# A tile of its own for a half result, and operand sums one weight block later

## The chip, the cores and the metric

One core of a Trainium2 chip runs the whole kernel. The metric is device time in microseconds (us) of one execution. TensorE (PE) multiplies, VectorE (DVE) and ScalarE (ACT) do elementwise work and read PSUM, GpSimd (POOL) does elementwise work on SBUF, and SyncE (SP) and ScalarE issue the DMAs.

## The reference

One decoder layer on 1024 tokens of width 1024, in float32: two token mixers side by side, gated and merged, then a gated MLP with a causal convolution of width 3.

```python
xn = rmsnorm(x, norm_mix_w)
da_q, da_k, da_v, sw_q, sw_k, sw_v, g_da, g_sw = split_cols(xn @ w_in)
y_da = diff_attention(da_q, da_k, da_v, lam, lam_init, subln_w)   # 4 heads, causal
y_sw = sliding_window_attention(sw_q, sw_k, sw_v, sinks)          # 8 heads, window 128
merged = sigmoid(g_da) * (y_da @ w_br_da) + sigmoid(g_sw) * (y_sw @ w_br_sw)
x = x + merged @ w_mix_out
xn = rmsnorm(x, norm_ffn_w)
u = xn @ w_up
c = conv_b + sum(shift(u, 2 - j) * conv_w[j] for j in range(3))
gate, val = split(c)
x = x + (silu(gate) * val) @ w_down                               # 2816 hidden columns
out = rmsnorm(x, norm_final_w)
```

## The kernel before

Activations lie transposed, channels on partitions and tokens along the free dimension; a product makes a 128x512 PSUM bank (128 output channels, half of the tokens). To keep float32 accuracy each operand is split into a high part (a cast to fp32r on ScalarE) and a low part (source minus high, on VectorE), and a product takes three matmuls: high by high, low by high, high by low. Weights come in blocks of 128 output channels: a DMA on SP into a tile "raw" (three buffers), a cast to "wh" (L132, two buffers), a low part "wl" (L134). `next_w` hands out the next block and prepares the one behind it. Some products use Strassen-Winograd's seven products for a two by two block product; their operands are sums and differences of weights (on GpSimd) and of activations (on VectorE).

The kernel is traced as one program by a framework that inserts all waits. It also chooses each engine's order before the run: of the instructions that it expects to be ready it takes the one traced first, so work can pass work that was traced ahead of it. Tiles of one pool and tag share that tag's buffers. `tc.issue_after(ins)` adds edges: what its block traces on the engine of `ins` is queued behind `ins`.

**The second attention** (`sw_step`, called from `attention` for units u = 4 and 5, eight steps each) takes four heads of 128 queries against two key blocks. A step makes scores (L707), a minimum and exponentials (L714, L716), a scaling (L721), transposes (L728), splits (L731, L732) and the value product (L738) into one PSUM bank. That product's lower 64 partitions hold the high parts of the values, the upper 64 the low parts; the upper half is copied by ScalarE to a tile (L740) and added to the lower one by VectorE in two instructions (L745) into "ys", which goes to memory.

Between the steps `back_half` works on the gates' projections that are left over: a half is 24 matmuls (L153 to L155) into one of two PSUM banks of the tag "g", a copy by ScalarE (L548) to an SBUF tile of the tag "g", and a DMA to memory. HALVES says how many halves follow each step (one behind steps 0, 2, 4, 6 of u = 4 and behind 2, 4, 6 of u = 5, four more behind the attention). The tile for L740 is of the same pool and tag as the gates' tile: two buffers in all. The first attention's norm (`da_norm`) keeps squares in a tile of the tag "sq" of the pool `ap`, one buffer, 512 elements wide. Behind the attention `rest` reads the results back ("yr", split into "yh" and "yl" by L806 and L807) and multiplies them by the branch weights.

**The down product** (`down`) takes 22 hidden row blocks j. The first 6 go as ordinary products in 16 pieces (L1083). The next 8 go as Strassen-Winograd products: four weight blocks m = 0..3 with B11 and B21 (the loop around L1112, on L887), then for each of four pairs the five products with T1, T2, B22, T3 and T4. The last 8 are ordinary again (L1056). `sums_h(k)`, for k = 0..3, loads four 128x512 pieces "hr" (L980, nine buffers), makes four differences in place on VectorE (L996, L998, L999, L1002) and splits them into T1 to T4 (cast L806, low part L807). `preps` are the splits of the operands that need no sum. The sums are traced at the last piece (k = 0) and behind the weight blocks m = 0, 1, 2 (k = 1, 2, 3). The weight that is prepared while block m is handed out is block m + 1, and for m = 3 the half weight A22.

Of the kernel before, what the change touches and what calls it, by code (L numbers as in the profile page):

```python
# [17 lines left out]
P = 128  # L18
# [24 lines left out]
class Trunk:  # L43
# [652 lines left out]
    def sw_step(self, g, n, st):  # L696
        nc, ap = self.nc, self.ap
        q, k = st
        k0 = max(n - 1, 0) * P
        w = P if n == 0 else 256  # L700
        bo = T + (P if n == 0 else 0)
        sc = self.tl(self.psS, [P, 4, 256], "sc")
        s = self.tl(self.st, [P, 4, 4], "sw", bufs=4)
        L = self.tl(ap, [P, 4, 256], "L", bufs=4)
        for h in range(4):
            for part in range(2):
                nc.tensor.matmul(sc[:, h, :], q[h][:, n * P:(n + 1) * P], k[part][:, k0:k0 + 256], start=part == 0, stop=part == 1)  # L707


        a, at, we = (0, w, w + 1) if n == 0 else (1, 0, w)  # L710
        nc.gpsimd.tensor_copy(L[:, :, at:at + 1], self.nsink[:, 4 * g:4 * g + 4].unsqueeze(2))
        for h in range(4):
            slope, ns = 2.0 ** -(4 * g + h + 1), self.nsink[:, 4 * g + h:4 * g + h + 1]
            nc.vector.tensor_tensor_reduce(L[:, h, a:w], sc[:, h, a:w], self.bias[:, bo + a:bo + w], slope, ns, ALU.add, ALU.min, s[:, 0, h:h + 1])  # L714
        for h in range(4):
            nc.scalar.activation(L[:, h, :we], L[:, h, :we], AF.Exp, bias=s[:, 0, h:h + 1], scale=-1.0, accum_out=s[:, 2, h:h + 1])  # L716
        nc.vector.reciprocal(s[:, 3, :], s[:, 2, :])
        if n:
            nc.gpsimd.memset(L[:, :, 0:1], 0.0)
        for h in range(4):  # L720
            self.last = nc.vector.tensor_scalar(L[:, h, a:w], L[:, h, a:w], s[:, 3, h:h + 1], None, ALU.mult)  # L721
        po = self.tl(self.psT, [P, H2], "t")
        nblk = w // P
        parts = []
        for b in range(nblk):
            ps = self.tl(self.psT, [P, 4, P], "t")
            for h in range(4):
                nc.tensor.transpose(ps[:, h, :], L[:, h, b * P:(b + 1) * P], self.ident)  # L728
            pt = self.tl(ap, [P, 2, 4, P], "aT", F32R, bufs=5)
            hi, lo = pt[:, 0], pt[:, 1]  # L730
            nc.scalar.copy(hi, ps)  # L731
            nc.vector.tensor_tensor(lo, ps, hi.bitcast(F32), ALU.subtract)  # L732
            parts.append((hi, lo))
        for b, (hi, lo) in enumerate(parts):
            kb = k0 // P + b
            va = self.vsw[kb // 4][:, kb % 4, g]
            for m, pt in enumerate((hi, lo)):
                nc.tensor.matmul(po, va, pt, start=b == 0 and m == 0, stop=b == nblk - 1 and m == 1)  # L738
        t = self.tl(self.gpool, [P, 4, P], "g", bufs=2)[0:64]
        nc.scalar.copy(t, po[64:128].rearrange("p (h q) -> p h q", h=4))  # L740
        pv = po[0:64].rearrange("p (c e q) -> p c e q", c=2, e=2)
        tv = t.rearrange("p (c e) q -> p c e q", e=2)
        y = self.tl(ap, [P, 2, P], "ys", bufs=3)
        for e in range(2):
            nc.vector.tensor_tensor(y[64 * e:64 * e + 64], pv[:, :, e], tv[:, :, e], ALU.add)  # L745
        self.store(self.yd[4 + 2 * g:6 + 2 * g, :, n * P:(n + 1) * P].rearrange("c p q -> p c q"), y)
# [288 lines left out]
    def down(self):  # L1035

        nc, tc = self.nc, self.tc
        with ExitStack() as ctx:
# [28 lines left out]
            sums = [lambda k=k: self.sums_h(k) for k in range(4)]  # L1067
            pss = {}
            n = N1 // 2
            for i, (m, c) in enumerate(self.pieces):  # L1070
                if i % 2 == 0:
                    with tc.high_priority(150 if i < 4 else 0):
                        w2 = self.next_w()
                w = [v[:, i % 2 * n:i % 2 * n + n] for v in w2]
                lo = self.lo
                for hf in range(2):
                    if c == 0:
                        pss[m, hf] = bank(hf)
                    js = range(n * c, n * c + n)
                    for q, j in enumerate(js):  # L1080
                        h, l = self.hs[hf, j]
                        for p, (v, x) in enumerate(((w[0], h), (w[0], l), (w[1], h))):
                            nc.tensor.matmul(pss[m, hf], v[:, q, :], x, start=c == q == p == 0, stop=c == 1 and q == n - 1 and p == 2 and (m > 3 or hf > 0))  # L1083
                if i in (2, 8):
                    ms = slice(4 - i // 8 * 4, 8 - i // 8 * 4)
                    nc.sync.dma_start(x3[:, ms], self.x2d[ms].rearrange("m p t -> p m t"))
                for _ in range(n if i < 2 else 1):
                    if preps:
                        preps.pop(0)()
                if i in DEFER:  # L1090
                    self.defer.pop(0)(lo)
                if i in STORE:

                    with tc.issue_after(self.load.ins):
                        self.late.pop(0)()
                if i == len(self.pieces) - 1:
                    sums.pop(0)()
                if c == 1:

                    for hf in range(m < 4, 2):  # L1100
                        x = col(m, hf)
                        tt(x, x, pss[m, hf], ALU.add)
            assert not preps
            ys = []
            for m in range(4):
                wh, wl = self.next_w()
                y, ps = bank(1), pss[m, 0]
                ys.append(y)
                self.product(y, (wh[:, 0:4], wl[:, 0:4]), "B11", skip=True, low=True)
                self.product(ps, (wh[:, 4:8], wl[:, 4:8]), "B21", first=False)  # L1110
                for p in (y, ps):
                    tt(col(m, 0), col(m, 0), p, ALU.add)  # L1112
                if sums:
                    sums.pop(0)()
            late = [(hf, j) for hf in range(2) for j in range(N1 + 8, NF)]
            for m, y in enumerate(ys):
                w = self.next_w()
# [23 lines left out]
            def evac(ps, m, hf, a=0, b=H2):  # L1141

                x = x3[:, m, hf * H2 + a:hf * H2 + b]
                tt(x, x, ps, ALU.add)
                sum_ = acc[:, hf, a:b]
                sq = sum_ if m == 0 else self.tl(self.uw, [P, b - a], "sl")
                nc.scalar.activation(sq, x, AF.Square)
                if m and (m < KC - 1 or not hf):
                    tt(sum_, sum_, sq, ALU.add)
                nc.scalar.mul(x, x, self.vecs[:, C_NO + m:C_NO + m + 1])  # L1150
                return sq
# [15 lines left out]
            for a, b in ((0, q), (q, H2)):  # L1167
                for m, w in ws:
                    ps = bank(m % 2)[:, :q]
                    mms(ps, w, 1, js, a, b, lambda n, m=m: tail.pop(0)() if a and n == (4 if m < KC - 1 else 2) else None)  # L1170
                    sq = evac(ps, m, 1, a, b)
# [100 lines left out]
```

## Time and profile before

| | |
|---|---|
| median of 3 runs | 1345.15 us (1344.61 to 1345.49) |
| the profiled execution | 1344.88 us, span 1343.0 us |
| granted TensorE clock, mean | 0.997 |
| PE busy | 1326.8 us, 99% |
| DVE busy | 1052.5 us, 78% |
| ACT busy | 602.3 us, 45% |
| POOL busy | 488.8 us, 36% |
| HBM | 133 GB/s over the span |

Profile times count from the first instruction of the span. The second attention's steps run from about 400 to 490 us, the branch products behind them from 502, the pieces of down from about 1099 and its four blocks of B11 and B21 from 1164.6. In a row of the profile "y<-h,wh" means: writes tile y, reads h and wh. The engine names PEld and SPq stand for TensorE's weight loads and SyncE's queue.

### The profile page before, as it was taken

What the parts mean: (1) busy time and instruction counts of PE and PEld (TensorE: products, weight loads), DVE (VectorE), ACT (ScalarE), POOL (GpSimd) and SP (SyncE); (2) the same over time, 40 slices, a digit from 0 to 9 for tenths busy, and PEclk for the clock granted to TensorE, in tenths of its full rate; (3) what the DMA queues carried; (4) which work ended last, traced back from release to release, by engine and by line L of the source; (5) the groups of instructions that cost most, each with busy time, mean ns of one, the idle gap of its engine ahead of it and who ended that gap; (6) DMA issues with size and microseconds to landing.
All of it is one profiled execution on the core that took longest, in us unless ns stands there. A gap on an engine that the chain in (4) does not pass through costs nothing.

```text
span 1343.0 us, 17167 instructions
## 1 busy us (share of the span) xinstructions
PE 1326.8 (99%) x6304; PEld 1105.7 (82%) x6304; DVE 1052.5 (78%) x1425; ACT 602.3 (45%) x929; POOL 488.8 (36%) x364
## 2 busy tenths in 40 slices
PE   8999999999999999999999999999999999999997
PEld 6888888888888878888888888888888888788886
DVE  7846775388898976445669999999999998967454
ACT  8432232276667774344444434343434345432433
POOL 0346652000101016642446566666666611131011
PEclk9999999999999999999999999999999999999998
DMA  7244443966554245324522222222222239642342
GB/s 258 108 146 162 148 149 119 273 170 189 143 148 144 70 155 206 141 95 130 167 79 95 79 79 85 88 79 79 88 85 80 86 128 320 220 145 98 94 141 79
DMA packets 63812, 179.49 MB, mean 134 GB/s; under 512 B 7024, under 2 KB 16880, under 8 KB 63728
## 3 DMA queue, kind: packets, MB, share of 16 engines
q1 hardware_dynamic: 52272, 161.22, 36.8%
q10 hardware_dynamic: 11456, 17.18, 3.5%
q8 instruction: 50, 0.82, 0.2%
q14 instruction: 34, 0.28, 0.1%
HBM read 129.61 MB, written 48.76 MB: 133 GB/s over the span
## 4 chain that ended last, share of the span: by engine, by line
PE 72%; DVE 15%; issue 8%; DMA 2%; ACT 1%; POOL 1%; SPq 0%; POOLq 0%; DVEq 0%; ACTq 0%
PE t L887 24%; PE g L153 4%; PE g L154 4%; PE g L155 4%; DVE c L1031 3%; PE y L1056 3%; PE d L1056 3%; PE sc L154 3%; PE sc L155 3%; PE sc L153 3%; PE d L887 3%; PE sc L619 3%; PE y L887 2%; DVE wl L113 2%; DMA hr<-hd 2%
## 5 line engine op out<-in xcount | busy, mean ns | idle before, releaser
L1020 POOL TENSOR_TENSOR us<-us,rstd 128x1024 f32<-128x1024 f32 x42 | 92.6, 2225 | 85.0 <-DVE us L452 47.6
L1029 ACT ACTIVATE c<-us,vecs 128x1024 f32<-128x1024 f32 x44 | 54.8, 1248 | 118.3 <-POOL us L1020 113.8
L132 ACT CAST wh<-raw 128x1024 fp32r<-128x1024 f32 (+2 forms) x58 | 58.7, 1012 | 107.9 <-PE sc L154 35.8
L134 DVE TENSOR_TENSOR wl<-raw,wh 128x1024 fp32r<-128x1024 f32 (+2 forms) x58 | 78.3, 1352 | 32.5 <-ACT wh L132 22.8
L113 DVE TENSOR_TENSOR sl<-sf,sh 128x1024 fp32r<-128x1024 f32 x62 | 89.3, 1442 | 12.8 <-ACT sh L111 12.8
L111 ACT CAST sh<-sf 128x1024 fp32r<-128x1024 f32 x62 | 64.5, 1042 | 61.6 <-PE t L887 44.0
L97 POOL TENSOR_TENSOR sf<-rv 128x512 f32<-128x512 f32 x30 | 51.3, 1711 | 93.6 <-DVE sl L113 51.1
L1031 DVE SCALAR_TENSOR_TENSOR c<-us,vecs,c 128x1024 f32<-128x1024 f32 x44 | 75.4, 1746 | 2.7 <-ACT c L1029 2.7
L99 POOL TENSOR_TENSOR sf<-raw,rv 128x512 f32<-128x512 f32 x30 | 56.7, 1891 | 46.3 <-DVE sl L113 46.3
L1032 DVE SCALAR_TENSOR_TENSOR c<-us,vecs,c 128x1024 f32<-128x1024 f32 x44 | 73.2, 1696 | 0.0
L153 PE MATMUL g<-xh,wh 128*128 128x512 f32 x176 | 71.0, 403 | 1.5 <-ACT g L548 1.5
L154 PE MATMUL g<-xl,wh 128*128 128x512 f32 x176 | 70.3, 400 | 0.0
L155 PE MATMUL g<-xh,wl 128*128 128x512 f32 x176 | 70.3, 399 | 0.0
L170 POOL TENSOR_TENSOR rs<-ms,mhalf 128x8 f32<-128x8 f32 (+2 forms) x9 | 13.5, 1499 | 155.5 <-DVE ms L168 149.4
L1012 ACT ACTIVATE c<-c 128x1024 f32<-128x1024 f32 x22 | 23.4, 1064 | 89.6 <-DVE c L1032 89.6
L113 DVE TENSOR_TENSOR wl<-raw,wh 128x1024 fp32r<-128x1024 f32 (+1 forms) x35 | 61.8, 1765 | 0.3 <-ACT wh L111 0.2
L602 POOL MEMSET aT<- 128x128 f32 x32 | 6.1, 204 | 151.5 <-PE t L648 101.2
L623 DVE CUSTOM_DVE_ANT_0 L<-sc,bias 128x128 f32<-128x128 f32 (+7 forms) x64 | 47.8, 752 | 16.6 <-PE sc L619 13.7
L98 POOL TENSOR_TENSOR sf<-sf,raw 128x512 f32<-128x512 f32 x31 | 58.2, 1877 | 2.2
L624 ACT ACTIVATE L<-L,sm 128x128 f32<-128x128 f32 (+7 forms) x64 | 49.6, 778 | 20.0 <-DVE sm L623 17.3
L776 POOL TENSOR_TENSOR gr<-gr,rstd 128x1024 f32<-128x1024 f32 x16 | 40.3, 2523 | 43.9 <-DMA gr<-gd 43.7
L113 DVE TENSOR_TENSOR wl<-rv,wh 128x512 fp32r<-128x512 f32 x30 | 54.0, 1800 | 2.6 <-ACT wh L111 2.6
(435 smaller groups left out, 4338.4 us busy)
## 6 DMA issues: line engine op xcount, KB each, us to landing
u<-qd SPq DMA_DIRECT2D x72, 256.0 KB, 6.4
raw<-in_w_down SPq DMA_DIRECT2D x27, 512.0 KB, 3.7
hr<-hd SPq DMA_DIRECT2D x50, 256.0 KB, 4.8
raw<-in_w_up SPq DMA_DIRECT2D x23, 512.0 KB, 3.5
raw<-in_w_in SPq DMA_DIRECT2D x22, 512.0 KB, 3.8
hd<-c SPq DMA_DIRECT2D x22, 512.0 KB, 2.6
rv<-in_w_up SPq DMA_DIRECT2D x21, 512.0 KB, 3.5
gr<-gd SPq DMA_DIRECT2D x16, 512.0 KB, 3.4
```

What stands on the lines that cost most here:

```text
L111: cast = nc.scalar.copy(hi, src)
L113: low = nc.vector.tensor_tensor(lo, src, hi.bitcast(F32), ALU.subtract)
L132: self.hi = nc.scalar.copy(wh, raw)
L134: self.lo = (eng or nc.vector).tensor_tensor(wl, raw, wh.bitcast(F32), ALU.subtract)
L153: nc.tensor.matmul(ps, wh[:, kc + o, :], ah, start=first and n == 0, stop=False)
L154: nc.tensor.matmul(ps, wh[:, kc + o, :], al, start=False, stop=False)
L155: nc.tensor.matmul(ps, wl[:, kc + o, :], ah, start=False, stop=last and n == len(kcs) - 1)
L887: nc.tensor.matmul(ps, (ah, ah, al)[p][:, k, :], (bh, bl, bh)[p], start=first and n == p == 0, stop=last and p == 2 and n == len(ks) - 1, ...
L1020: i = (nc.vector if m % NF == 0 else nc.gpsimd).tensor_tensor(us[:, 2:], us[:, 2:], self.rstd, ALU.mult)
L1031: nc.vector.scalar_tensor_tensor(c, us[:, 1:T + 1], cw[1], c, ALU.mult, ALU.add)
L1032: nc.vector.scalar_tensor_tensor(c, us[:, 0:T], cw[0], c, ALU.mult, ALU.add)
L1056: nc.tensor.matmul(ps, v[:, n, :], x, start=n == i == 0, stop=n == len(js) - 1 and i == 2)
```

## The change

In `sw_step` the tile for the half result comes from the pool `ap` under the tag "sq" with one buffer, where it came from the gates' pool under the tag "g" with two. In `down` the sums for k = m are traced at the beginning of the weight block m, behind `next_w` and ahead of its products; none is traced at the last piece. Each block of sums is put behind `self.hi`, the cast of the weight prepared last, which concerns its casts on ScalarE alone.

```diff
@@ sw_step
-        t = self.tl(self.gpool, [P, 4, P], "g", bufs=2)[0:64]
+        t = self.tl(ap, [P, 4, P], "sq", bufs=1)[0:64]
         nc.scalar.copy(t, po[64:128].rearrange("p (h q) -> p h q", h=4))
@@ down
                         self.late.pop(0)()
-                if i == len(self.pieces) - 1:
-                    sums.pop(0)()
                 if c == 1:
...
             for m in range(4):
                 wh, wl = self.next_w()
+
+                with tc.issue_after(self.hi.ins):
+                    sums.pop(0)()
                 y, ps = bank(1), pss[m, 0]
                 ys.append(y)
                 self.product(y, (wh[:, 0:4], wl[:, 0:4]), "B11", skip=True, low=True)
                 self.product(ps, (wh[:, 4:8], wl[:, 4:8]), "B21", first=False)
                 for p in (y, ps):
                     tt(col(m, 0), col(m, 0), p, ALU.add)
-                if sums:
-                    sums.pop(0)()
```

## The prediction

> **What bounds the kernel now.** I read the page first, then the waits of TensorE over the whole span, then the timelines of the two places that the change touches. The page's first row, and the waits view (who waited for whom: total us, times, longest us):
>
> ```profile
> PE 1326.8 (99%) x6304; PEld 1105.7 (82%) x6304; DVE 1052.5 (78%) x1425; ACT 602.3 (45%) x929; POOL 488.8 (36%) x364
> ```
> ```profile
> PE t L280 <- ACT wh L310: 5.0, 1, 5.0
> PE g L153 <- ACT g L548: 1.5, 4, 0.5
> ...
> PE y L887 <- DVE wl L134: 0.5, 1, 0.5
> PE t L738 <- DVE aT L732: 0.4, 1, 0.4
> PE y L887 <- ACT wh L132: 0.3, 1, 0.3
> ...
> PE d L1083 <- DVE wl L134: 0.2, 1, 0.2
> PE t L728 <- DVE ys L745: 0.2, 1, 0.2
> ```
>
> TensorE is busy 99% of the span, so a change that neither adds nor removes matmuls can gain only what TensorE waits. The first row above is the kernel's start, which the change does not touch. The others shown lie in the two places that it does touch: the second attention (L153 on g, L738, L728) and the first part of down (L1083, L887). Together they are 3.1 us. That is the stock from which a gain can come; a loss has no such limit.
>
> **The first edit: the half result's tile.** The columns of a timeline are start, busy time, engine, line, operation, and in brackets the idle time before it with what ended it.
>
> ```profile
> 410.11 0.58 ACT L740 COPY g<-t 64x512 f32<-64x512 f32 x1 [1.49 <-PE t L738]
> 410.72 0.59 ACT L548 COPY g<-g 128x512 f32<-128x512 f32 x1
> ...
> 487.91 0.58 ACT L740 COPY g<-t 64x512 f32<-64x512 f32 x1 [1.51 <-DMA yd<-ys]
> ...
> 488.58 0.59 ACT L548 COPY g<-g 128x512 f32<-128x512 f32 x1
> ```
> ```profile
> 411.36 0.50 PE L153 MATMUL g<-xh,wh 128*128 128x512 f32 x1 [0.25 <-ACT g L548]
> ...
> 484.61 0.50 PE L153 MATMUL g<-xh,wh 128*128 128x512 f32 x1 [0.50 <-ACT g L548]
> ...
> 509.93 0.39 PE L153 MATMUL g<-yh,wh 128*128 128x512 f32 x1
> ```
>
> Between 408 and 490 us ScalarE makes eight gate copies (L548), and each stands directly behind a half-result copy (L740); the first and the last pair are shown. Both write a tile of the tag "g", two buffers handed out in program order, and in the program the gate's tile follows the step's. So a finished gate half sits in its PSUM bank until the step's last matmul (L738) is done and L740 has run. There are two such banks; four times TensorE needs one back and waits, 1.5 us in all by the waits view, 0.25 the first time and 0.50 the last. With the half result in a tile of its own, L548 can go as soon as its half is ready, and these four waits go.
>
> A wait costs more than the idle time shown, because a matmul's modelled end lies behind the moment at which the next could start. The row of eight at 1164.58 (below) takes 1.98 us, a single one 0.39 (509.93 above): (1.98 - 0.39) / 7 = 0.227 us from start to start, so 0.39 - 0.23 = 0.16 us of the last one's time is normally overlapped and is lost at each wait. I take the same tail for the transposes and score matmuls that precede these waits. The edit is worth 1.5 + 4 x 0.16 = 2.1 us.
>
> The edit also adds a wait: the new tag has one buffer, so L740 must follow the two adds (L745) that read the half result of the step before. Below are the two that stand nearest to each other in the rows that I read, and the last reader of the same tag in the stage before:
>
> ```profile
> 405.14 0.95 PE L161 MATMUL t<-ones,sq 128*128 128x1 f32 x8
> ```
> ```profile
> 448.22 0.85 DVE L745 TENSOR_TENSOR ys<-t,g 64x256 f32<-64x256 f32 x2
> ```
> ```profile
> 451.17 0.58 ACT L740 COPY g<-t 64x512 f32<-64x512 f32 x1 [0.38 <-PE t L738]
> ```
>
> The adds end at 449.07, the next copy starts at 451.17: 2.1 us of cover, so I cost this at nothing. If VectorE fell behind by more than that, each excess would stand on ScalarE ahead of the casts and exponentials queued there. The tag is the one in which the first attention's norm keeps its squares; their last reader, L161, ends at 406.1, so the first step's copy at 410.11 finds it free.
>
> What comes next when TensorE stops waiting? The sixteen steps keep VectorE busy too:
>
> ```profile
> 408.00:490.00 82.00, 79.97 (x452) 66.25 (x451) 74.33 (x240) 59.44 (x161) 8.29 (x27) 1.00 0.36 116
> ```
> ```profile
> 505.25 2.44 DVE L807 TENSOR_TENSOR yl<-yr,yh 128x1024 fp32r<-128x1024 f32 x2 [0.69 <-ACT yh L806]
> ```
>
> In the windows view the columns behind the length are the busy times of TensorE (79.97 of 82), its weight loads, VectorE (74.33), ScalarE and GpSimd. So the steps may end no sooner than now, near 489 us, and the gain appears only as less gate work left over behind them. That work hides the trip of the last result through memory. Its last low part ends at 505.25 + 2.44 = 507.69 and its first reader is the fourth row block of the branch product, at 509.93: 2.24 us of slack. If the trip doesn't move at all, 2.1 of gain still fits, barely. The other two waits of this stage (L738, L728: 0.4 and 0.2, with tails 0.9 us) come from VectorE and I leave them in.
>
> **The second edit: the operand sums.** Rows of ScalarE, TensorE, VectorE, GpSimd and the SP queue, one of the windows view, and two of the page's DMA rows (size, median us to landing):
>
> ```profile
> 1139.33 0.62 ACT L806 CAST h<-hr 128x512 fp32r<-128x512 f32 x1 [2.09 <-DVE hr L996]
> ...
> 1148.45 4.27 ACT L806 CAST h<-hr 128x512 fp32r<-128x512 f32 x8
> ...
> 1161.56 1.04 ACT L132 CAST wh<-raw 128x1024 fp32r<-128x1024 f32 x1
> 1167.08 2.40 ACT L806 CAST h<-hr 128x512 fp32r<-128x512 f32 x4 [4.48 <-DVE hr L999]
> 1169.39 1.04 ACT L132 CAST wh<-raw 128x1024 fp32r<-128x1024 f32 x1
> ...
> 1176.82 1.06 ACT L132 CAST wh<-raw 128x1024 fp32r<-128x1024 f32 x1 [0.36 <-ACT wh L132]
> 1182.22 0.62 ACT L132 CAST wh<-raw 128x512 fp32r<-128x512 f32 x1 [4.34 <-PE d L887]
> ```
> ```profile
> 1164.58 1.98 PE L887 MATMUL y<-h,wh 128*128 128x512 f32 x8
> ...
> 1170.48 2.11 PE L887 MATMUL y<-h,wh 128*128 128x512 f32 x8 [0.30 <-ACT wh L132]
> 1173.05 1.20 PE L887 MATMUL y<-h,wl 128*128 128x512 f32 x4 [0.45 <-DVE wl L134]
> ...
> 1189.73 0.61 PE L887 MATMUL d<-h,sh 128*128 128x512 f32 x2
> ```
> ```profile
> 1156.53 2.88 DVE L807 TENSOR_TENSOR h<-hr,h 128x512 fp32r<-128x512 f32 x2
> ...
> 1168.16 2.49 DVE L807 TENSOR_TENSOR h<-hr,h 128x512 fp32r<-128x512 f32 x4
> ...
> 1183.05 0.69 DVE L134 TENSOR_TENSOR wl<-raw,wh 128x512 fp32r<-128x512 f32 x1
> ```
> ```profile
> 1157.13 1.73 POOL L98 TENSOR_TENSOR c<-c,raw 128x512 f32<-128x512 f32 x1
> ...
> 1185.19 1.31 POOL L97 TENSOR_TENSOR c<-raw 128x512 f32<-128x512 f32 x1 [24.63 <-DMA raw<-in_w_down]
> ```
> ```profile
> 1190.00:1200.00 10.00, 10.00 (x46) 8.29 (x45) 5.12 (x8) 2.11 (x2) 3.27 (x3) 1.00 0.31 107
> ```
> ```profile
> 1151.93 0.33 SPq L122 DMA_DIRECT2D raw<-in_w_down  x1
> ```
> ```profile
> raw<-in_w_down SPq DMA_DIRECT2D x27, 512.0 KB, 3.7
> hr<-hd SPq DMA_DIRECT2D x50, 256.0 KB, 4.8
> ```
>
> The 512 KB weights of the four blocks are cast by the 128x1024 rows of L132, the first at 1161.56, the second at 1169.39, the fourth at 1176.82; the row at 1182.22 is the half weight behind them. The second was asked for at 1151.93 and landed near 1155.6; its buffer came free when the last piece ended, at 1164.58. Yet its cast ran at 1169.39, because ScalarE stood 4.48 us before a cast of an operand sum, L806, that waited for VectorE's subtraction L999. TensorE paid 0.30 for the high part and 0.45 for the low part. The change orders every cast of a block's sums behind the cast of the next weight, so this cast can run at 1164.6 and its low part a microsecond later, against needs at 1170.0 and 1171.8. Both waits go: 0.30 + 0.45 + 2 x 0.16 = 1.1 us. The wait at L1083 (0.24 in its row, 0.40 with the tail) may go as well, since the first operand's low part leaves the gapless VectorE row ahead of it; I leave it out of the sum and use it as the lower end.
>
> What moves: of the sixteen sum operands, one is cast at 1139.33 and eight at 1148.45. These nine now come behind 1164.6. The casts have room (ScalarE idles 4.3 us before 1182.22). Their low parts cost VectorE 2.49 / 4 = 0.62 each, 5.6 us in all, in a stretch where it runs without a gap until 1183.7 (the last row of it is shown) and idles about half the time behind (5.12 busy of 10 from 1190). So its queue would be worked off near 1189.3, and the last block's first operand, with three low parts behind it, would be done near 1187.4. Its reader is the fourth k of the first product, at 1189.73 now and 1188.6 with 1.1 us saved: 1.2 us of slack by this bound. The bound from the other side takes no backlog: the last block's casts stand behind the cast at 1182.22 (1181.1 after the gain), so cast and low part end by 1181.1 + 0.62 + 0.62 + 0.69 = 1183.0, with 5.6 us of slack. I take the middle, on time, because low parts are traced ahead of the adds and can pass them.
>
> The loads of the sums stay on SP in the same program order, but nine buffers hold them. With two blocks' sums waiting, the third's loads now wait for the first's low parts, near 1167 to 1169, the fourth's for the second's, near 1174.5. With 4.8 us to landing that is 1179 to 1180, in time for casts at 1181. Weights queued behind these loads on SP are needed later still.
>
> One row asks for care: two low parts at 1156.53 took 2.88 us, where the rate above gives 1.2, while GpSimd was adding. The Trainium skill, page "SBUF — State Buffer", section "Who interferes with whom", says that a VectorE instruction with two SBUF inputs and a GpSimd instruction that reads SBUF exclude each other for the whole instruction. By it the moved low parts would be quicker where GpSimd now rests, but slower if they met its next sums, at 1185; the trace agrees as far as that one row goes.
>
> **The sum.** Against the profiled execution's 1344.88 us (span 1343.0, so 1.9 around it): 1344.88 - 2.1 - 1.1 = 1341.7. The median of the three runs is 0.3 above that execution, so the forecast is 1341.9. From TensorE's last wait here to the end the chain is matmuls without a gap, so what is saved arrives.
>
> **The rivals.** *One edit alone pays.* Either the steps are paced by VectorE, and the gate copies again meet the half-result copies in ScalarE's queue, or the weight's low part stands behind subtractions on VectorE. Then the gain is 1.1 or 2.1, that is 1344.0 or 1343.0. For: VectorE is gapless in both places. Against: each wait that TensorE pays has another engine's order, not its load, ahead of it.
>
> *Nothing moves.* The pairs of copies fall together because the half's matmuls and the step's end together, and the sums' waits turn up at the next weight: 1345.1. Against: eight pairs out of eight, and a weight that lay ready 4.8 us.
>
> *The operands come late: slower.* The engines' queues are fixed before the run. If a subtraction of the third or fourth block stands on VectorE ahead of a weight's low part and its load, now asked for later, has not landed, everything behind it waits, as ScalarE did for 4.48 us. Or the last block's first operand misses 1188.6. A load's 4.8 us on top of the exhausted 1.2 of slack, a subtraction and a split (three steps of 0.6) give a stall of 4.8 + 1.8 - 1.2 = 5.4 us; with 2.1 gained in the attention and the 1.1 not, the time is 1345.15 - 2.1 + 5.4 = 1348.4. It decides from the point at which that operand's low part ends behind 1188.6. For: nine operands move into VectorE's fullest stretch, and the buffers tie loads to them. Against: the stretch has half its time free behind 1183.7.
>
> **How the numbers follow.** A measurement of this kernel can tell about 0.2%, 2.7 us, from no change: faster means below 1342.5, slower above 1347.8. The forecast has 0.50, of which 0.03 ends short of 2.7; one edit alone 0.22; nothing 0.09; late operands 0.19, of which 0.03 stay mild. So faster 0.47, same 0.37, slower 0.16. The lower end takes the forecast with the waits at L1083, L738 and L728 gone too: 1341.9 - 0.4 - 0.9 = 1340.6. The upper end, 1347.8, leaves out the 0.16 of late operands that are not mild; about 0.03 lies below the lower one. The forecast's own range is 1340.6 to 1343.0.
>
> **What would show it.** In the changed profile: L548 no longer behind each L740, and no row of TensorE on g waiting for L548; the second weight's cast of the four blocks near 1162 us (1164.6 less the 2.1 gained) with no L806 waiting in front of it; no L887 wait on the first block of the sums' products. A row of TensorE waiting for h L807 or for VectorE's wl in the four blocks would make the second term wrong; a longer idle time at the first products on yh would take back the first.

## The result, and the profile after

| | before | after |
|---|---|---|
| median | 1344.61 us (1343.36 to 1345.49, 9 runs) | 1348.22 us (1346.69 to 1349.18, 9 runs) |
| profiled execution | 1344.88 us, span 1343.0 us | 1348.7 us, span 1346.9 us |
| granted TensorE clock, mean | 0.997 | 0.995 |

The ratio is 1.0027 (95% interval 1.0018 to 1.0036): 3.6 us slower, where 1341.9 us was forecast. The page's first row and the waits of TensorE (who waited for whom: total us, times, longest us), changed kernel:

```profile
PE 1326.9 (99%) x6304; PEld 1105.6 (82%) x6304; DVE 1054.8 (78%) x1425; ACT 602.2 (45%) x929; POOL 486.4 (36%) x364
```
```profile
PE t L280 <- ACT wh L310: 5.6, 1, 5.6
PE g L154 <- DVE yl L807: 4.8, 1, 4.8
...
PE d L887 <- DVE h L807: 0.4, 1, 0.4
...
PE d L1083 <- DVE wl L134: 0.3, 1, 0.3
```

The waits on L548, L738 and L728 and both of L887 for the weight are gone. One new wait of 4.8 us, of the branch product's low by high matmul (L154) for the last result's low part (yl), is longer than everything that went. The first wait, at the kernel's start, which the change does not touch, was 5.6 us in this execution and 5.0 in the one before.

ScalarE at the first step, changed kernel (start, busy time, engine, line, operation):

```profile
408.61 0.59 ACT L548 COPY g<-g 128x512 f32<-128x512 f32 x1
...
410.19 0.58 ACT L740 COPY sq<-t 64x512 f32<-64x512 f32 x1 [0.98 <-PE t L738]
```

The gate copy no longer stands behind the half-result copy here; of the seven gate copies between 400 and 490 us only the one at 420.95 still does. TensorE, VectorE and GpSimd where the branch product begins, changed kernel:

```profile
507.04 0.39 PE L153 MATMUL g<-yh,wh 128*128 128x512 f32 x1
512.27 0.79 PE L154 MATMUL g<-yl,wh 128*128 128x512 f32 x1 [4.85 <-DVE yl L807]
512.87 0.63 PE L155 MATMUL g<-yh,wl 128*128 128x512 f32 x1
...
517.56 0.44 PE L154 MATMUL g<-yl,wh 128*128 128x512 f32 x1
...
518.07 0.39 PE L153 MATMUL sc<-yh,wh 128*128 128x512 f32 x1
```
```profile
501.81 3.79 DVE L807 TENSOR_TENSOR yl<-yr,yh 128x1024 fp32r<-128x1024 f32 x3 [4.70 <-ACT yh L806]
505.53 3.41 DVE L134 TENSOR_TENSOR wl<-raw,wh 128x1024 fp32r<-128x1024 f32 x1
508.86 3.35 DVE L807 TENSOR_TENSOR yl<-yr,yh 128x1024 fp32r<-128x1024 f32 x1
```
```profile
505.43 5.71 POOL L776 TENSOR_TENSOR gr<-gr,rstd 128x1024 f32<-128x1024 f32 x2 [3.31 <-DMA gr<-gd]
```

The matmul at 507.04 is the one that stood at 509.93 before: TensorE arrives 2.89 us earlier. Then TensorE needs the last low part, and that lies behind something else. Before, VectorE's queue had all the results' low parts first (ending at 507.69) and the second branch weight's low part (L134) behind them:

```profile
507.61 3.44 DVE L134 TENSOR_TENSOR wl<-raw,wh 128x1024 fp32r<-128x1024 f32 x1
```

In the changed kernel the two have changed places, and both run beside GpSimd's two multiplications of gates (L776), at 3.4 us each where three low parts just ahead took 3.79 together. The last low part ends at 512.21.

The wait also costs speed. From 512.87 to 517.56 the matmuls start (517.56 - 512.87) / 11 = 0.426 us apart, where the usual distance is 0.227. The windows view (length, busy times of the five engines, granted TensorE clock, DMA share, GB/s), changed kernel:

```profile
507.00:512.00 5.00, 0.43 (x2) 0.00 (x1) 5.00 (x2) 1.07 (x2) 4.14 (x2) 0.88 0.46 132
512.00:517.00 5.00, 4.73 (x11) 3.76 (x12) 2.04 (x3) 0.00 (x0) 0.00 (x0) 0.50 0.23 93
517.00:522.00 5.00, 5.00 (x22) 4.03 (x22) 3.57 (x2) 2.48 (x3) 2.40 (x1) 0.93 0.00 0
```

From the matmul at 507.04 to the first on "sc", at 518.07, are 15 starts and 11.03 us; 15 x 0.227 = 3.40, so 7.63 us are lost: 4.85 + 0.16 for the wait with its tail, and 2.6 for the granted clock of 0.50 behind it. Against 2.89 gained, this place alone makes the kernel 4.74 us slower. In down 0.66 us are gained (TensorE's excess, defined below, between 1100 and 1220 us), which leaves 4.1; the span grew by 3.9.

In down, ScalarE, VectorE and TensorE of the changed kernel:

```profile
1169.04 1.05 ACT L132 CAST wh<-raw 128x1024 fp32r<-128x1024 f32 x1 [3.04 <-PE y L1083]
1170.00 2.17 ACT L806 CAST h<-hr 128x512 fp32r<-128x512 f32 x4
```
```profile
1187.31 1.20 DVE L134 TENSOR_TENSOR wl<-raw,wh 128x512 fp32r<-128x512 f32 x1
1188.43 1.77 DVE L996 TENSOR_TENSOR hr<-hr,hr 128x512 f32<-128x512 f32 x1
1190.13 0.67 DVE L1113 TENSOR_TENSOR x<-x,y 128x512 f32<-128x512 f32 x1
1190.72 1.18 DVE L998 TENSOR_TENSOR hr<-hr,hr 128x512 f32<-128x512 f32 x1
1191.83 1.77 DVE L807 TENSOR_TENSOR h<-hr,h 128x512 fp32r<-128x512 f32 x1
```
```profile
1193.66 0.50 PE L887 MATMUL d<-h,sh 128*128 128x512 f32 x1 [0.40 <-DVE h L807]
```

The second weight's cast (1169.04) runs as soon as its buffer is free, with no L806 in front, and the blocks' products (from 1169.07 in this trace) start without a wait. But the last block's first operand comes 0.40 us late at its reader, the fourth row block of the first of the five products. Two subtractions (L996, L998) and its low part (L807) are stretched, up to 1.77 us where one of each usually takes 0.68 to 0.69 in the kernel before, beside GpSimd's sums of weights. L1113 between them, which reads one of its inputs from PSUM, is not stretched (0.67):

```profile
1186.66 1.29 POOL L97 TENSOR_TENSOR c<-raw 128x512 f32<-128x512 f32 x1 [22.70 <-DMA raw<-in_w_down]
...
1189.62 1.74 POOL L98 TENSOR_TENSOR c<-c,raw 128x512 f32<-128x512 f32 x1
1191.44 1.61 POOL L100 TENSOR_TENSOR c<-raw,c 128x512 f32<-128x512 f32 x1
```

### The profile page after: what moved, and what is told of

The parts are those of the page before. It is cut to its first block, busy times and chain, and to the rows that moved or that the text cites. A ratio compares the mean times of both kernels' runs of the same rounds, so it can differ in the third digit from the quotient of the medians.

```text
span 1346.9 us, 17159 instructions
## 1 busy us (share of the span) xinstructions
PE 1326.9 (99%) x6304; PEld 1105.6 (82%) x6304; DVE 1054.8 (78%) x1425; ACT 602.2 (45%) x929; POOL 486.4 (36%) x364
## 4 chain that ended last, share of the span: by engine, by line
PE 48%; DVE 7%; issue 3%; DMA 2%; ACT 1%; POOL 0%; SPq 0%; POOLq 0%; DVEq 0%; ACTq 0%
PE t L887 23%; PE y L1056 3%; PE d L1056 3%; PE sc L154 3%; PE sc L155 3%; PE sc L153 3%; PE d L887 2%; PE y L887 2%; DMA hr<-hd 2%; DVE c L1031 2%; PE g L154 1%; PE g L155 1%; PE g L153 1%; DVE c L1032 1%; DVE wl L134 1%
## 5 line engine op out<-in xcount | busy, mean ns | idle before, releaser
L134 DVE TENSOR_TENSOR wl<-raw,wh 128x1024 fp32r<-128x1024 f32 (+2 forms) x58 | 78.3, 1352 | 32.3 <-ACT wh L132 22.6
L111 ACT CAST sh<-sf 128x1024 fp32r<-128x1024 f32 x62 | 64.5, 1042 | 61.5 <-PE t L887 44.0
L154 PE MATMUL g<-xl,wh 128*128 128x512 f32 x176 | 71.1, 404 | 0.0
L776 POOL TENSOR_TENSOR gr<-gr,rstd 128x1024 f32<-128x1024 f32 x16 | 39.4, 2465 | 43.0 <-DMA gr<-gd 42.9
```

What stands on the lines that cost most here:

```text
L111: cast = nc.scalar.copy(hi, src)
L134: self.lo = (eng or nc.vector).tensor_tensor(wl, raw, wh.bitcast(F32), ALU.subtract)
L154: nc.tensor.matmul(ps, wh[:, kc + o, :], al, start=False, stop=False)
```

## The experiments

All times are medians; each ratio is to runs of the kernel before on the same chip (medians 1344.87 us for the first four experiments, 1345.01 for the next four, 1345.15 for the last two). One measure used below is worked out from the traces: TensorE's excess, the sum by which the distances from start to start of its matmuls exceed the usual ones, in slices of 20 us. A slice without a wait comes out at 0.06.

**Each edit alone.** The first run keeps the line of `sw_step` and puts the sums back; the second does the reverse.

```diff
 first edit alone
-        t = self.tl(self.gpool, [P, 4, P], "g", bufs=2)[0:64]
+        t = self.tl(ap, [P, 4, P], "sq", bufs=1)[0:64]
 second edit alone
-                if i == len(self.pieces) - 1:
-                    sums.pop(0)()
+                with tc.issue_after(self.hi.ins):
+                    sums.pop(0)()
-                if sums:
-                    sums.pop(0)()
```

> The first edit alone (the half result's tile), the sums as before. Theory A, the loss is at the branch products (VectorE prepares the second branch weight's low part ahead of the last attention result's low part, both slowed beside GpSimd): the wait of about 5 us on g for yl and the halved clock behind it are here too, and the sums' gain of 0.6 us is missing: about 4.2 us slower than before. Rival B, the loss is the late operands of down: about 2.9 us faster than before.

> The second edit alone (the sums one block later), the tile as before. Theory A: the two waits at the weight blocks (1.3 us with their tails) go, a wait for h L807 of 0.8 comes at the first sums' product: 0.6 us faster than before, within what can be told. Rival B: slower by 3 us or more.

The first edit alone: 1348.36 us, ratio 1.0028 (1.0018 to 1.0038), all of the loss. The second alone: 1345.54 us, 1.001 (1.0001 to 1.0018), neither the 0.6 us faster nor the 3 us slower that were expected. VectorE and TensorE's wait with the first edit alone:

```profile
505.15 3.43 DVE L134 TENSOR_TENSOR wl<-raw,wh 128x1024 fp32r<-128x1024 f32 x1
508.50 3.35 DVE L807 TENSOR_TENSOR yl<-yr,yh 128x1024 fp32r<-128x1024 f32 x1
```
```profile
511.91 0.50 PE L154 MATMUL g<-yl,wh 128*128 128x512 f32 x1 [4.47 <-DVE yl L807]
```

The swapped pair is there without any change in down, and the slice from 500 us has an excess of 6.4 us against 0.06 before. With the second edit alone the pair stands in the old order; the slices at 1160 and 1180 go from 1.40 and 0.06 to 0.06 and 1.16: most of what the weight's wait gave back, the operand's lateness took.

**The order of the two low parts, and GpSimd.** Two runs change one thing each in the changed kernel. One queues the second branch weight's split behind the last result's; the other lets GpSimd's first four multiplications of gates (blocks m = 0 and 1) wait for the last result's low part and leaves VectorE's order to the planner, the part of the framework that chooses the order.

```diff
 order
+                last_y = self.lo
                 for m in range(KC):
-                    w = self.next_w()
+                    with nullcontext() if m else tc.issue_after(last_y.ins): w = self.next_w()
 GpSimd
                         i = nc.gpsimd.tensor_tensor(g, g, self.rstd, ALU.mult)
+                        if m < 2: (i waits for last_y)
```

> The changed kernel, with one edge: the second branch weight's low part is queued behind the last result's low part on VectorE. Theory A: the wait of 5 us on yl falls to 0 to 2 us, too short for the clock to halve, so 5 to 7.6 us less than the changed kernel: 3 us faster than before, near 1341.5. Rival B: no change against the changed kernel.

> The changed kernel, with GpSimd's gate multiplications of the first two branch blocks made to wait for the last result's low part; this changes VectorE's and ScalarE's order at that place a little too. Theory A, if GpSimd's part in it is what makes the two VectorE operations take 3.4 us each: they take 1.2 each, the wait for yl falls from 5 us to under 1, near 1341.5. If the order alone counts: a wait of 2 to 4 us stays. Rival B: no change against the changed kernel.

With the order: 1342.58 us, 0.9989 (0.998 to 0.9998), 5.6 us below the changed kernel by the medians. Three of its eleven runs took 1345.95 to 1347.04 us, and the two longest of them had a mean clock of 0.996 where the others had 0.997 or 0.998; of these no trace was kept. Its VectorE rows, TensorE's wait and the window behind it:

```profile
505.95 2.25 DVE L807 TENSOR_TENSOR yl<-yr,yh 128x1024 fp32r<-128x1024 f32 x1
508.12 3.42 DVE L134 TENSOR_TENSOR wl<-raw,wh 128x1024 fp32r<-128x1024 f32 x1
```
```profile
508.25 0.50 PE L154 MATMUL g<-yl,wh 128*128 128x512 f32 x1 [0.76 <-DVE yl L807]
```
```profile
512.00:517.00 5.00, 5.00 (x24) 4.08 (x23) 1.87 (x3) 1.96 (x3) 3.24 (x1) 1.00 0.32 105
```

In the profiled execution the wait falls from 4.85 to 0.76, the clock stays at 1.00, and the slice's excess is 1.32. The edge moved three more things: one VectorE instruction (L787, a multiplication of gates) went ahead of the last low part, which makes that part later; two matmuls of TensorE went ahead of the wait, which covers 0.45 us; and two DMAs on SP changed places. So the order of the pair gives all but about half a microsecond of the shorter wait.

With GpSimd held back the weight's low part still runs ahead of the last result's, and yet there is no wait at this place. VectorE and then TensorE's waits for the 115 us behind it:

```profile
501.36 1.23 DVE L134 TENSOR_TENSOR wl<-raw,wh 128x1024 fp32r<-128x1024 f32 x1 [0.21 <-ACT wh L132]
502.50 3.49 DVE L807 TENSOR_TENSOR yl<-yr,yh 128x1024 fp32r<-128x1024 f32 x3
```
```profile
PE g L153 <- DVE gr L792: 2.4, 4, 1.0
```

The weight's low part that took 3.41 takes 1.23. It also runs 4.2 us earlier, ahead of three results' low parts where it stood ahead of one, so this run does not show GpSimd's part by itself. An estimate from the rows: in the changed kernel's order and undisturbed, the pair would take 2.35 us (506.27 to 508.62 in the run with the finer hold, below) from 505.53 and end at 507.9, 0.6 us behind its reader's turn at 507.27. The time is 1345.7 us, 1.0003 (0.9994 to 1.0012): the held gates arrive late, so the PSUM banks that are emptied with them come free late, and TensorE waits four times for one. This gives most of the gain back.

**The same without the second edit, and a finer hold of GpSimd.** The next pair has the first edit and the order edge with the sums at their old places; in the second of them the multiplications of one block (m = 1) also wait for the last low part. The order on every engine is the same in both, so they differ in GpSimd's time alone.

> The first edit with the edge on VectorE (second branch weight's low part behind the last result's), the sums as before. If the sums edit is worth little or a slight loss, as its own run showed: 2.9 us gained in the steps less 1.3 of wait left at the branch products, 1.6 faster than before, near 1343.3, the same as the edge with both edits. If the sums edit gave the gain there: near 1344.9.

> The kernel with the first edit and the edge, and GpSimd's two gate multiplications of the second branch block alone made to wait for the last result's low part; the order on every engine stays the same. Theory A (GpSimd's reads slow that low part from 1.2 to 3.4 us): it takes 1.2, the 1.3 us left at the branch products go, near 1342.0; the second block's gates start 3 us later, which its own 3 us of rest on GpSimd covers. If the low part stays at 3.4 us, GpSimd's part in it is refuted.

Without the hold 1342.78 us, 0.9984 (0.9975 to 0.9993); with it 1342.92 us, 0.9981 (0.9972 to 0.999). The last result's and the weight's low part, first without the hold, then with it:

```profile
506.17 2.25 DVE L807 TENSOR_TENSOR yl<-yr,yh 128x1024 fp32r<-128x1024 f32 x1
508.34 3.41 DVE L134 TENSOR_TENSOR wl<-raw,wh 128x1024 fp32r<-128x1024 f32 x1
```
```profile
506.27 1.22 DVE L807 TENSOR_TENSOR yl<-yr,yh 128x1024 fp32r<-128x1024 f32 x1
507.40 1.22 DVE L134 TENSOR_TENSOR wl<-raw,wh 128x1024 fp32r<-128x1024 f32 x1
```
```profile
507.56 5.69 POOL L776 TENSOR_TENSOR gr<-gr,rstd 128x1024 f32<-128x1024 f32 x2 [5.89 <-DVE yl L807]
```

So GpSimd's presence is what stretches these instructions: 2.25 and 3.41 us with it, 1.22 and 1.22 when it starts behind the first of them (the second had begun 0.16 us ahead of it). The excess at 500 us falls from 1.28 to 0.07, but 0.99 appears between 580 and 600 (0.06 without the hold), of which one row shows a wait of 0.19 us for the last block's low part (ml, L797) behind the held gates; the time is the same.

**A gate half kept back.** In the changed kernel one gate half of the last unit is left for behind the attention (five there instead of four), to see whether more work there covers the trip of the last result.

```diff
-HALVES = (..., (0, 0, 1, 0, 1, 0, 1, 0), (4,))
+HALVES = (..., (0, 0, 1, 0, 1, 0, 0, 0), (5,))
```

> The changed kernel, with one gate half more kept for behind the attention (five in place of four; the one behind the last unit's step 6 is taken from there). Theory A as a question of cover: 5.4 us more work hide the last result's way through memory and the wait for yl goes, but the last steps have less to fill TensorE with; 5 us or more less than the changed kernel if those steps idle under 2 us. If the order on VectorE alone decides: the same wait as in the changed kernel, 4 us slower than before.

1344.04 us, 1.0 (0.999 to 1.0009). TensorE has the same work in all ahead of the branch product, and reaches its tenth matmul at 506.89, hardly earlier than the 507.04 of the changed kernel. The wait is shorter all the same, 1.66 us. TensorE, VectorE and GpSimd:

```profile
508.94 0.50 PE L154 MATMUL g<-yl,wh 128*128 128x512 f32 x1 [1.66 <-DVE yl L807]
```
```profile
504.33 1.22 DVE L134 TENSOR_TENSOR wl<-raw,wh 128x1024 fp32r<-128x1024 f32 x1
505.47 3.41 DVE L807 TENSOR_TENSOR yl<-yr,yh 128x1024 fp32r<-128x1024 f32 x1
```
```profile
504.63 6.52 POOL L776 TENSOR_TENSOR gr<-gr,rstd 128x1024 f32<-128x1024 f32 x2 [3.69 <-DMA gr<-gd]
```

The order is still the wrong one, but L134 began 0.30 us ahead of GpSimd's first multiplication and got through in 1.22 us; only the second of the pair is stretched. This is one execution: the eleven runs lie from 1342.05 to 1348.72 us, the three longest, from 1346.36 on, with a mean clock of 0.995 or 0.996, as in most runs of the changed kernel. Whether L134 lost its lead there is not shown.

**The sums: their order, their place, their edge.** With the second edit alone, the sums k = 3 are traced ahead of the last weight's preparation (A22), so that their first operand might pass its low part:

```diff
             for m in range(4):
-                wh, wl = self.next_w()
+                if m < 3: wh, wl = self.next_w()
                 with tc.issue_after(self.hi.ins):
                     sums.pop(0)()
+                if m == 3: wh, wl = self.next_w()
```

> The second edit alone, with the last block's sums (k = 3) traced ahead of the half weight A22 in place of behind it. If that weight's low part and cast in front of the last sums make the first product wait (1.1 us with its tail in the second edit's own profile): the wait is under 0.4, near 1344.2, 1.3 us below the second edit alone. If VectorE's backlog or the loads make it: no change, near 1345.5.

1347.04 us, 1.0019 (1.0008 to 1.0029), worse than the second edit as it is. The wait at the first of the five products is gone, but the products behind it wait (TensorE's waits of this run):

```profile
PE y L887 <- DVE x L1122: 3.8, 2, 2.8
```
```profile
1187.29 5.18 DVE L807 TENSOR_TENSOR h<-hr,h 128x512 fp32r<-128x512 f32 x3
```
```profile
1197.70 0.62 ACT L806 CAST h<-hr 128x512 fp32r<-128x512 f32 x1 [7.08 <-DMA hr<-hd]
```

Three low parts took 5.18 us beside GpSimd's sums of weights (four of them, 1182.51 to 1191.92), where four took 2.49 before, and ScalarE stood 7.08 us before a cast whose piece had not landed. No run separates the two, but the trace has a chain for the longer wait: VectorE idled 5.01 us before 1200.47 for a cast (L111) that stands behind that late cast on ScalarE, and then worked without a gap until L1122 had run, at 1211.91.

Two more runs ask whether the place in the text or the edge makes the operand late. The first has the first edit, the order edge and the finer hold as above, with the sums at their old places, and queues only the sums k = 2 and 3 behind the cast of the second weight (the text below calls them the third and fourth sum of each block). The other is the second edit alone without its edge.

```diff
 queue only
-                wh, wl = self.next_w()
+                wh, wl = self.next_w(); h1 = h1 if m else self.hi.ins
...
                 if sums:
-                    sums.pop(0)()
+                    with tc.issue_after(h1) if m else nullcontext(): sums.pop(0)()
 place only
+                wh, wl = self.next_w()
+                sums.pop(0)()
```

> First edit with the edge that keeps the second branch weight's splits behind the last result's, GpSimd's multiplication of the one block m = 1 behind that result as in the run with 1342.92 us, and the sums at their old place in the text; only the third and fourth sum of each block are queued behind the cast of the second weight's high part. Theory (the waits for the weight at the first products go once the casts of the operand sums leave their queue place ahead of the weight's cast, and the operand is in time as long as its loads are issued early): the two waits at L887, 1.4 us with their tails, are gone, no wait of a product for h or x, about 1341.5 us, runs as close together as those of that earlier run. Rival (any later place of these casts makes the operand late): a wait at the fourth product of 0.4 us or more, 1343 to 1345 us and runs that lie further apart.

> Second edit alone, without its queue edge: the sums k = 2, 3 are written behind the first weight block as in the changed kernel, but nothing holds their casts behind the second weight's cast. Theory (the edge makes the operand late): no wait of the fourth product for its operand, slice 1180 at 0.1 us of excess; the waits for the weight stay away or return, so 1343.5 to 1344.9 us. Rival (the later place in the text does it, since it puts A22's low part and the h loads' adds first on VectorE): the 0.4 us wait and its tail stay, about 1345.5 us, and the runs lie as far apart as with the edge.

Queue only: 1342.35 us, 0.9978 (0.997 to 0.9987), the lowest ratio here, though not clear of the 0.9981 of the run without its edge; place only: 1345.23 us, 1.0001 (0.9992 to 1.001). ScalarE in the first, then in the second:

```profile
1163.87 1.06 ACT L132 CAST wh<-raw 128x1024 fp32r<-128x1024 f32 x1 [1.69 <-PE y L1083]
```
```profile
1168.28 2.40 ACT L806 CAST h<-hr 128x512 fp32r<-128x512 f32 x4 [4.49 <-DVE hr L999]
1170.59 1.04 ACT L132 CAST wh<-raw 128x1024 fp32r<-128x1024 f32 x1
```

With the edge on k = 2 and 3 the weight's cast leaves at 1163.87 and both waits at L887 are gone (slices at 1160 and 1180: 0.08 and 0.06); its runs lie 2.1 us apart, those of the run without its edge 2.3. Without the edge the sums' casts stand ahead of the weight's cast again, as before the change (4.49 us of standing, 4.48 before), the two waits are back (0.6 and 0.5 us), L1083 waits 1.0 us for its weight where it waited 0.2 before, and no operand is late. So the edge is what removes the weight's waits. The operand is late in no run without the edge on every block; no run has that edge with the sums at their old places, so whether it or the place together with it makes the operand late is not shown. The median of the first is 0.6 us below that of the run without its edge, not the 1.4 expected; the profiles' difference near 1160 is 1.35, and 0.9 of it is lost between 580 and 600 (1.91 against 0.99; a wait of 0.80 us for L792), where the two kernels do not differ in the text, nor their engines in order. Whether that belongs to the execution or to the kernel the runs don't say.

## Why the prediction was wrong, point by point

**The copies and the gate waits: right in mechanism, too small in size.** L548 left its place behind L740 and the four waits are gone. The waits at L738 and L728, which the prediction left in at 0.9 us with tails, went as well, and no run tells why: TensorE waits for nothing between 395 and 500 us. The gain ahead of the branch product is 2.89 us, not 2.1 (2.1 + 0.9 = 3.0). The cover of the one-buffer tile held.

**The slack of the last result's trip: the step that failed.** The prediction took the low part's end, 507.69, and its first reader, 509.93, and let 2.24 us of slack carry a gain of 2.1, "barely". That matmul reads yh; the one that reads the low part is L154 behind it, 0.23 us later, so the slack was 2.47. With 2.9 gained it would have been used up in any case; at 0.4 us short that would have been little. The trip itself moved as little as the prediction allowed for: the last high part's cast (L806) ends at 506.05, where it ended at 506.43. What it missed is that the slack was measured against an end that belongs to one queue order. The planner sets VectorE's order anew when anything moves, and the weight's low part, until then directly behind the last result's, came in front of it. That row (507.61, 3.44 us) does not appear in the prediction; its place behind the last low part was taken for granted. Its 3.4 us, the stretch of the last low part from 1.2 to 3.35, and the slow clock behind the wait are the loss. The runs bear on each of the three: the order edge takes the wait from 4.85 to 0.76 us; without GpSimd beside it a part of 3.4 us takes 1.2; and with a wait of 0.76 us the clock stays at 1.00, so the 2.6 us come with the long wait.

**The sums: half right.** The two L887 waits for the weight went as predicted (1.40 to 0.06 in their slice). The operand, given 1.2 us of slack by the backlog bound, came 0.40 us late. The bound counted low parts at 0.62 us; beside GpSimd the two subtractions (L996, L998) and the low part took 1.77, 1.18 and 1.77. The prediction saw the same meeting in its own trace (two low parts in 2.88 us), said that the moved ones would be slower "if they met its next sums, at 1185", and put no price on it; they met. The page it named there, "SBUF — State Buffer" of the Trainium skill, section "Who interferes with whom", bore on the branch products far more than on the place where it was applied: the pair of runs with equal order and 2.25 and 3.41 against 1.22 and 1.22 us shows the effect it states. The second edit's worth was put at 1.1 us gained; alone it measures 0.5 us slower (interval of the ratio 1.0001 to 1.0018). The profiles give 0.2 us gained at the place itself. In this run's profiled execution TensorE's last matmul ends 0.84 us earlier than before (1336.26 against 1337.10), yet the span is 0.3 us longer: the last output lands 4.4 us after its DMA is issued, where it took 2.9. Whether the other executions share that is not shown, and the cause of the 0.5 us stays open.

**The rivals.** "Operands come late" named nearly the measured time, 1348.4, but that is luck. Its stall of 5.4 us came from a load's 4.8 us in down, where the lateness is 0.4 us and comes from GpSimd; the measured loss lies in the branch products, where no load is late. What it had right is the kind of cause: a low part that stands on VectorE behind work queued ahead of it. The chance of 0.16 for slower and an upper end of 1347.8 were too low, because slack in a replanned queue was booked as safe.

**What would have shown it** was named: "a longer idle time at the first products on yh".

## What to carry to other kernels

When the engine that sets the time is freed, the next hand-off to it decides, and the slack there holds only as long as the order of the queue that feeds it: list what stands next to the critical instruction on its engine and price a swap with each neighbour, by its longest row. Where orders are planned anew, the fix for such a loss is an edge of order on the one pair; the same first edit that cost 3.5 us gains 2.2 with it. A wait as long as the 4.85 us here must be priced with the slow matmuls behind it, 2.6 us more.

## What the runs showed of the hardware

An idle time of 4.85 us is followed by about 5 us at a granted clock of 0.50, with matmuls 0.426 us apart. With the first edit alone 4.47 us of idle time are followed by only 3.4 us of it, from 0.6 us behind the wait on (windows of 1 us there show 0.75, 0.50, 0.50, 0.55 from 512 to 516, then 1.00): nearly the same wait, and an excess of 6.4 against 7.6 us. Behind the 0.76 us of the run with the order edge, and behind the 2.84 us of the run with the reordered sums, the clock is 1.00; that run's wait and the window behind it:

```profile
1212.63 0.73 PE L887 MATMUL y<-h,sh 128*128 128x512 f32 x2 [2.84 <-DVE x L1122]
```
```profile
1212.00:1217.00 5.00, 4.37 (x19) 3.63 (x20) 3.62 (x6) 1.06 (x1) 2.59 (x2) 1.00 0.73 252
```

The Trainium skill, page "TensorE: Matmul & The Clock Gate", section "What's actually happening", says that TensorE falls to half rate after at least one idle window of about 3.4 us and returns after about as long a time of work. The rows of 2.84, 4.47 and 4.85 us agree; where between 2.84 and 4.47 us the limit for one wait lies, no run here shows. One wait is not the only way to the slow clock: at the end of the kernel before, where TensorE waits 0.84 and 1.09 us between a few short matmuls, the clock is 0.50 as well:

```profile
1336.00:1338.00 2.00, 1.10 (x4) 0.70 (x4) 1.29 (x3) 0.37 (x1) 0.41 (x1) 0.50 0.38 134
```

A VectorE subtraction of 128x1024 with both inputs in SBUF takes 1.22 us alone and 2.25 to 3.44 us beside GpSimd's multiplications, and those take up to 6.65 us for two where one alone takes 2.40 (the row at 519.38 of the run with the order edge):

```profile
519.38 2.40 POOL L776 TENSOR_TENSOR gr<-gr,rstd 128x1024 f32<-128x1024 f32 x1 [3.27 <-DMA gr<-gd]
```

Which of the two starts first decides who is stretched: 0.30 us of lead was worth 2.2 us to L134. The rows fit engines that take turns, each instruction waiting until the other engine's has ended. An estimate for the changed kernel by that rule: GpSimd's first multiplication from 505.43 to 507.83, L134 to 509.05 (measured 508.94), GpSimd's second to 511.45 (511.14), the last low part to 512.67 (512.21). So the price of such a meeting is what is left of the other engine's instruction, up to 2.40 us here.
